# Two blocks on one core: the second blocks' softmax division on ScalarE, and merged masks in the third branch

## The chip, the cores and the metric

The kernel runs on one core of a Trainium2 chip. The metric is the device time of one launch in microseconds. Engines are called as in the profile: PE (TensorE, matmuls; PEld its weight loads), DVE (VectorE), ACT (ScalarE), POOL (GpSimd), SP (the queue that issues most DMAs).

## The reference

The input has 512 tokens of width 1024 in float32. A first block (differential attention, multiscale pooling, a two-level mixture of experts) is followed by two layers of a second kind of block. Each of these layers projects the normed input and feeds three branches side by side: a gated delta rule ("gdn"), a latent attention with 6 heads ("mla") and a linear recurrence with decay ("rwkv", called the third branch here). Their outputs are gated, joined and multiplied with `w_out_2`, and added to the residual.

Two pieces of it matter here. The latent attention is, per head, softmax(q kT) v over 512 tokens. With blocks of 128 queries that is 4 x 6 = 24 units per layer, each with a 128x512 matrix of weights that is divided by its row sums. The third branch is computed in chunks of 64 tokens: inside a chunk, products of keys and queries with keys are masked to a triangle, and a unit lower triangular system of each chunk is solved.

## The kernel before, in words

After the first block (until about 1000 us) come the two layers, one after the other. The Python code that builds the program has generators for the branches; `weave` interleaves them, and what it settles is the order of PE's instructions, which is kept as it is written. The orders of DVE, ACT, POOL and SP come from the scheduler of the framework, which places each instruction where its own simulated times put it. So a change of one instruction's engine or size can move others on these engines. All engines run their instructions in order: one that waits holds up those behind it.

The stretch of the change is where the third branch's `prepare` and then its `states` are woven with `mla`.

*The third branch, `products` (L1922 to L1967).* For each of two directions and four token tiles, 16 small matmuls fill the PSUM tile `x2`, one half for each parity of head (`par`). DVE then writes `SC` (the products times the mask `mk`) and `RB` (the products times `m2`): before, one instruction for each parity, so four instructions a tile. 16 matmuls with `SC` follow, whose results ACT copies to `AKV` (L1963) and DVE adds to `YK` (L1967). There are 8 such tiles a layer, 16 in all. The last three of a layer lie inside the solve.

*The third branch, the solve (L1990 to L2006).* The triangular systems go through DRAM into the layout `au`, and DVE solves them by 30 pairs of instructions, `stmp` (L1342, a product of two parts of `au`) and `au` (L1344, a subtraction), each waiting for the one before. The solution goes through DRAM again into `XT` and `LT`, is transposed by DVE (L2004, L2006), and the matmuls of `off_diagonal` follow, then `states`.

*The latent attention (`mla`, L2152 on).* `scores(n)` for a unit: one matmul into a PSUM tile `mm`; DVE takes the negated row maximum `nm` (L2233); ACT computes `e = exp(scores + nm)` and the row sums `rs` (L2236, with a second small instruction that reads the sums out); DVE takes the reciprocal of `rs` (L2237); POOL multiplies `e` by it (L2238). `turn(n)` transposes the scaled `e` by four matmuls (L159), and ACT copies the result to `t2` (L2246). `outputs` multiplies `t2` of two heads with the values into `mo`. `scores` runs three units ahead of `turn`, and three PSUM tiles serve both in turn, so a new `scores` also needs an older `t2` copy to be done.

When the last unit is done, `Mix` takes over the memory of the attention and loads `w_out_2`, the gate and the branch outputs.

Of the kernel before, what the change touches and what calls it, by code (L numbers as in the profile page):

```python
# [12 lines left out]
AF = mybir.ActivationFunctionType  # L13
ALU = mybir.AluOpType
# [76 lines left out]
def half(p):  # L91
    return slice(64 * p, 64 * p + 64)
# [6 lines left out]
def tok(t):  # L99
    return slice(128 * t, 128 * t + 128)  # L100
# [1648 lines left out]
class Rwkv:  # L1749
# [54 lines left out]
    def prepare(self, mud, xud):  # L1804
        net, a, l, rw, tc, nc = self.net, self.a, self.l, self.rw, self.net.tc, self.net.nc
# [8 lines left out]
        RB = pl.tile([128, 2, 16, 64], F32, name="RB")  # L1814
# [6 lines left out]
        with pool(tc, "rka", 1, "right") as tmp, pool(tc, "rks", 2, "right") as small, pool(tc, "rpa", 1, "right", PSUM) as psum:  # L1821
# [102 lines left out]
            def products(d):  # L1924

                BB = BBs[d]
                m1 = net.const("stf64" if d == 0 else "stb64")
                m2 = net.const("inf64" if d == 0 else "inb64")
                mk = small.tile([128, 128], F32, name="mk", bufs=1)
                nc.gpsimd.tensor_copy(mk[:, 0:64], m1)  # L1930
                nc.gpsimd.tensor_copy(mk[:, 64:128], m2)
                for t in range(NT):
                    us = slice(4 * t, 4 * t + 4)
                    yield 1.2
                    ps = psum.tile([128, 2, 512], F32, name="x2", bufs=1)
                    for par in range(2):
                        for cp in range(2):
                            for i in range(2):
                                for c in range(2):
                                    o, f = cp * 192 + i * 64, 64 - 64 * i  # L1940
                                    ts = slice(t * 128 + c * 64, t * 128 + c * 64 + 64)
                                    net.matmul(ps[half(c), par, o:o + 128 - f], BB[half(par), i, cp, ts],
                                                     KR[half(par), d, cp, 2 * t + c, f:], start=True, stop=True)
                    pv = ps[:, :, :384].rearrange("p a (c k) -> p a c k", c=2)
                    SC = small.tile([128, 2, 2, 128], F32, name="SC")
                    for par in range(2):
                        nc.vector.tensor_tensor(SC[:, par], pv[:, par, :, 64:], mk[:, None, :].to_broadcast([128, 2, 128]), op=ALU.mult)
                    for par in range(2):
                        nc.vector.tensor_tensor(RB[:, d, us].rearrange("p (a c) k -> p a c k", a=2)[:, par], pv[:, par, :, 0:64],
                                                m2[:, None, :].to_broadcast([128, 2, 64]), op=ALU.mult)  # L1950
                    SU = SC.rearrange("p a c k -> p (a c) k")
                    yield 1.5
                    pv = psum.tile([128, 512], F32, name="mm", bufs=2)
                    for u in range(4):
                        h = 2 * (u % 2) + u // 2
                        for j in range(2):
                            for c in range(2):
                                net.matmul(pv[half(c), 256 * j + u * 64:256 * j + u * 64 + 64], SU[half(c), u, 64 * j:64 * j + 64],
                                           vt[half(c), t, h * 64:h * 64 + 64], start=True, stop=True)
                    pvv = pv.rearrange("p (x u k) -> p x u k", x=2, u=4)  # L1960
                    for c in range(2):
                        st = 2 * t + c if d == 0 else 7 - 2 * t - c
                        nc.scalar.activation(AKV[half(c), st], pvv[half(c), 0], AF.Copy)  # L1963
                    if d == 0:
                        nc.scalar.activation(YK[:, t], pvv[:, 1], AF.Copy)
                    else:
                        nc.vector.tensor_tensor(YK[:, t], pvv[:, 1], YK[:, t], op=ALU.add)  # L1967
# [42 lines left out]
            def rest():  # L2010
                yield from triangles(0)
                yield from products(0)
                while 1 not in BBs:
                    yield 1
                yield from products(1)
                yield from bonus()
# [132 lines left out]
def mla(net, a, l, mchd, mixt, tabd):  # L2149

    tc, nc = net.tc, net.nc
    with ExitStack() as ctx:  # L2152
# [75 lines left out]
        def scores(n):  # L2228
            t, h = units[n]
            ps = psum.tile([128, 512], F32, name="mm", bufs=3)  # L2230
            net.matmul(ps, qT[:, h, tok(t)], kT[:, h], start=True, stop=True)
            nm = tmp.tile([128, 1], F32, name="nm")
            nc.vector.tensor_reduce(nm, ps, AX.X, ALU.max, negate=True)  # L2233
            e = es[n] = tmp.tile([128, S], F32, name="e", tag="t1", bufs=4)
            rs = tmp.tile([128, 1], F32, name="rs")
            nc.scalar.activation(e, ps, AF.Exp, bias=nm, accum_out=rs)  # L2236
            nc.vector.reciprocal(rs, rs)  # L2237
            nc.gpsimd.tensor_scalar(e, e, rs, None, op0=ALU.mult)  # L2238

        def turn(n):  # L2240
            e = es.pop(n)
# [22 lines left out]
        for n in range(3):  # L2264
            scores(n)
        yield 0.8
        for n in range(len(units) + 1):
            if n < len(units):
                turn(n)
                yield 0  # L2270
            if n + 3 < len(units):
                scores(n + 3)
                yield 0
            if n and n % 2 == 0:
                outputs(n - 2)
                yield 0
# [262 lines left out]
```

## Time and profile before

| | us |
|---|---|
| median of 3 runs | 1907.91 |
| lowest and highest run | 1902.60, 1915.12 |
| the profiled execution's own time | 1903.25 |
| its span, first to last instruction | 1901.5 |
| busy: PE, DVE, ACT, POOL | 1653.5, 1046.3, 583.7, 558.4 |

A page of the profile gives busy times by engine, the chain of work that ended last, and the costliest groups of instructions with a mean time of one. The trace behind it can be asked for stretches of time (windows), for who waited for whom, and for instructions in order (timeline). A row like `L2238 POOL TENSOR_SCALAR e<-e,rs` names the line, the engine, the operation, and output and inputs by the program's names. "idle before <-X" is time in which the engine had nothing to run, and X what ended it.

### The profile page before, as it was taken

Reading aid. Unit: us, or ns where it says so; the run is one execution under the profiler, and the core shown is the slowest. Engines: PE = TensorE matmul, PEld = TensorE weight load, DVE = VectorE, ACT = ScalarE, POOL = GpSimd, SP = SyncE. Lnnn points to the kernel's source line nnn. Section 1 sums busy time; section 2 is a strip of 40 time slices with the busy share of each in tenths; the row PEclk is TensorE's granted clock in tenths of the full one; section 3 lists DMA queues with packets and bytes.
Section 4 is the critical chain, followed back from the end, with each engine's and each line's share of the span. In section 5 each row is a group of like instructions: output and inputs, shape, how many; then the busy total and the mean of one; then the engine's idle time right before and its main releaser. Section 6 shows DMA issues by size and latency. Waiting matters only on the chain.

```text
span 1901.5 us, 34119 instructions
## 1 busy us (share of the span) xinstructions
PE 1653.5 (87%) x14010; PEld 1100.7 (58%) x14010; DVE 1046.3 (55%) x2224; ACT 583.7 (31%) x1154; POOL 558.4 (29%) x559
## 2 busy tenths in 40 slices
PE   5999998999999999959978968777789799789776
PEld 3986584444444444438756755455577577545554
DVE  2435534344434333355895567836656875678456
ACT  4344432212121212144432124331344331244212
POOL 1113111000000000025651243454335721354443
PEclk8899998999999999979988989898889999989888
DMA  9934726999999999833424120123433441201332
GB/s 310 238 107 139 257 74 221 393 392 398 399 406 400 392 399 396 308 102 95 106 68 99 62 73 21 30 93 106 133 84 94 112 111 50 53 33 39 99 111 89
DMA packets 243219, 337.10 MB, mean 177 GB/s; under 512 B 92769, under 2 KB 166161, under 8 KB 226225
## 3 DMA queue, kind: packets, MB, share of 16 engines
q1 hardware_dynamic: 241152, 329.88, 50.3%
q10 hardware_dynamic: 1152, 3.22, 0.5%
q8 instruction: 112, 1.84, 0.4%
q0 software_dynamic: 752, 1.76, 0.3%
q14 instruction: 51, 0.41, 0.1%
HBM read 310.84 MB, written 23.99 MB: 176 GB/s over the span
## 4 chain that ended last, share of the span: by engine, by line
PE 25%; DVE 17%; DMA 5%; issue 4%; POOL 3%; ACT 2%; SPq 1%; DVEq 0%; POOLq 0%; ACTq 0%
PE mm L149 17%; DVE stmp L1342 2%; DVE au L1344 2%; PE mm L159 2%; PE tr L149 1%; PE x L149 1%; PE pu L149 1%; PE kp L149 1%; DMA w<-in_w_out_dram 1%; DMA au<-mud 1%; DVE nm L2233 1%; DVE y L1293 1%; PE mo L149 1%; DMA gate<-gated 1%; POOL w L2310 1%
## 5 line engine op out<-in xcount | busy, mean ns | idle before, releaser
L149 PE MATMUL gu<-w,XT 128*64 128x512 f32 x1024 | 225.8, 594 | 0.0
L149 PE MATMUL mm<-hh,wh 128*128 128x512 f32 (+1 forms) x464 | 203.9, 440 | 0.0
L149 PE MATMUL mm<-hh,wl 128*128 128x512 f32 (+1 forms) x464 | 188.4, 406 | 0.0
L149 PE MATMUL mm<-hl,wh 128*128 128x512 f32 (+1 forms) x464 | 188.1, 405 | 0.0
L928 POOL TENSOR_TENSOR yl<-y,yh 128x512 fp32r<-128x512 f32 x30 | 38.1, 1270 | 451.4 <-ACT yh L927 451.4
L149 PEld LDWEIGHTS gu<-w,XT 128*64 128x64 f32 x1024 | 72.1, 137 | 142.7 <-issue 136.2
L938 DVE TENSOR_TENSOR xres<-mm,xres 128x512 f32<-128x512 f32 x128 | 79.2, 681 | 90.7 <-PE mm L149 90.7
L149 PE MATMUL mm<-w,hT 128*64 128x512 f32 x512 | 113.4, 595 | 0.7 <-ACT hT L912 0.7
L149 PE MATMUL mm<-w,mh 128*128 128x512 f32 x256 | 92.9, 442 | 22.8 <-POOL w L2310 10.0
L149 PEld LDWEIGHTS mm<-hh,wh 128*128 128x128 f32 (+1 forms) x464 | 91.6, 198 | 26.6 <-issue 3.5
L149 PEld LDWEIGHTS mm<-hh,wl 128*128 128x128 f32 (+1 forms) x464 | 91.1, 196 | 21.0
L149 PEld LDWEIGHTS mm<-hl,wh 128*128 128x128 f32 (+1 forms) x464 | 91.8, 198 | 19.1 <-DVE hl L1162 0.2
L1214 ACT ACTIVATE wh<-w 128x1024 fp32r<-128x1024 f32 (+1 forms) x54 | 57.0, 1056 | 145.8 <-PE mm L149 105.9
L1216 POOL TENSOR_TENSOR wl<-w,wh 128x1024 fp32r<-128x1024 f32 (+1 forms) x28 | 69.4, 2478 | 110.0 <-ACT wh L1214 91.3
L149 PE MATMUL mm<-wh,hh 128*128 128x256 f32 x320 | 93.8, 293 | 2.2 <-ACT hh L357 2.2
L149 PE MATMUL mm<-wh,hl 128*128 128x256 f32 x320 | 91.0, 284 | 4.3 <-DVE hl L359 4.0
L2238 POOL TENSOR_SCALAR e<-e,rs 128x512 f32<-128x512 f32 x48 | 75.5, 1574 | 65.3 <-DVE rs L2237 59.8
L149 PE MATMUL mm<-wl,hh 128*128 128x256 f32 x320 | 90.6, 283 | 1.6 <-DVE wl L381 1.6
L149 PEld LDWEIGHTS mm<-w,hT 128*64 128x64 f32 x512 | 35.3, 137 | 66.6 <-issue 62.5
L149 PEld LDWEIGHTS mm<-w,mh 128*128 128x128 f32 x256 | 50.1, 206 | 41.1 <-POOL w L2310 12.5
L1342 DVE TENSOR_TENSOR stmp<-au 96x60 f32<-96x60 f32 (+29 forms) x120 | 64.5, 537 | 14.3 <-DMA au<-rmud 6.5
L872 ACT ACTIVATE X<-mm,ws 128x512 f32<-128x512 f32 x32 | 22.0, 688 | 151.4 <-DVE ws L869 128.1
(580 smaller groups left out, 3596.3 us busy)
## 6 DMA issues: line engine op xcount, KB each, us to landing
w<-in_w_gate_dram SPq DMA_DIRECT2D x64, 1024.0 KB, 13.2
w<-in_w_up_dram SPq DMA_DIRECT2D x64, 1024.0 KB, 13.4
w<-in_w_down_dram SPq DMA_DIRECT2D x64, 1024.0 KB, 10.0
w<-in_w_in_dram SPq DMA_DIRECT2D x52, 512.0 KB, 4.1
w<-in_w_ada_dram SPq DMA_DIRECT2D x24, 1024.0 KB, 8.5
w<-in_w_out_dram SPq DMA_DIRECT2D x16, 512.0 KB, 3.8
w<-in_w_in_dram SPq DMA_DIRECT2D x6, 1024.0 KB, 12.1
w<-in_w_out_dram SPq DMA_DIRECT2D x4, 1024.0 KB, 6.3
```

The costliest lines, as they stand in the source:

```text
L149: return self.nc.tensor.matmul(out, a, b, **kw)
L159: return self.nc.tensor.transpose(out, a, ident)
L872: nc.scalar.activation(X[:, 512 * i:512 * i + 512], ps, AF.Copy, scale=ws[:, 1:2])
L928: (nc.vector if last else nc.gpsimd).tensor_tensor(yl[:, hs], y, yh[:, hs].bitcast(F32), op=ALU.subtract)
L938: nc.vector.tensor_tensor(net.xres[:, t, hs], po, net.xres[:, t, hs], op=ALU.add)
L1214: nc.scalar.activation(h[:, :, :m], w[:, :, :m], AF.Copy)
L1216: eng.tensor_tensor(lo[:, :, :m], w[:, :, :m], h[:, :, :m].bitcast(F32), op=ALU.subtract)
L1293: nc.vector.scalar_tensor_tensor(y[:, lo:hi], ps[:, lo + d:hi + d], cw[:, j, m:m + 1], y[:, lo:hi], op0=ALU.mult, op1=ALU.add)
L1342: nc.vector.tensor_tensor(tv, au[:n, :, j + 1:, j:j + 1].to_broadcast(sh), au[:n, :, j:j + 1, 0:j].to_broadcast(sh), op=ALU.mult)
L1344: nc.vector.tensor_tensor(au[:n, :, j + 1:, 0:j], au[:n, :, j + 1:, 0:j], tv, op=ALU.add)
L2233: nc.vector.tensor_reduce(nm, ps, AX.X, ALU.max, negate=True)
L2238: nc.gpsimd.tensor_scalar(e, e, rs, None, op0=ALU.mult)
```

## The change

Two edits. In `products`, the two instructions for `SC` become one of 128x512 elements, and the two for `RB` one of 128x256. In `scores`, the multiplication of `e` by the reciprocal sums leaves POOL and becomes an ACT instruction, a copy with a scale of one value per partition, in place.

```diff
--- before.py
+++ after.py
@@ -1943,11 +1943,9 @@
                                                      KR[half(par), d, cp, 2 * t + c, f:], start=True, stop=True)
                     pv = ps[:, :, :384].rearrange("p a (c k) -> p a c k", c=2)
                     SC = small.tile([128, 2, 2, 128], F32, name="SC")
-                    for par in range(2):
-                        nc.vector.tensor_tensor(SC[:, par], pv[:, par, :, 64:], mk[:, None, :].to_broadcast([128, 2, 128]), op=ALU.mult)
-                    for par in range(2):
-                        nc.vector.tensor_tensor(RB[:, d, us].rearrange("p (a c) k -> p a c k", a=2)[:, par], pv[:, par, :, 0:64],
-                                                m2[:, None, :].to_broadcast([128, 2, 64]), op=ALU.mult)
+                    nc.vector.tensor_tensor(SC, pv[:, :, :, 64:], mk[:, None, None, :].to_broadcast([128, 2, 2, 128]), op=ALU.mult)
+                    nc.vector.tensor_tensor(RB[:, d, us].rearrange("p (a c) k -> p a c k", a=2), pv[:, :, :, 0:64],
+                                            m2[:, None, None, :].to_broadcast([128, 2, 2, 64]), op=ALU.mult)
                     SU = SC.rearrange("p a c k -> p (a c) k")
                     yield 1.5
                     pv = psum.tile([128, 512], F32, name="mm", bufs=2)
@@ -2235,7 +2233,7 @@
             rs = tmp.tile([128, 1], F32, name="rs")
             nc.scalar.activation(e, ps, AF.Exp, bias=nm, accum_out=rs)
             nc.vector.reciprocal(rs, rs)
-            nc.gpsimd.tensor_scalar(e, e, rs, None, op0=ALU.mult)
+            nc.scalar.activation(e, e, AF.Copy, scale=rs)
 
         def turn(n):
             e = es.pop(n)
```

The diff shifts line numbers by 2: the exp is L2234, the new ACT multiplication L2236 and the copy to `t2` L2244 in the changed program.

PE's order is the same in both programs, instruction for instruction. The schedulers' orders of the others differ. First ACT, in the first of the two layers, from the first exp of `mla` on. Before:

```order
L2236 ACTIVATE e_11016,rs_11017<-mm_11012,nm_11014 128x512
L2236 ACTIVATE e_11025,rs_11026<-mm_11021,nm_11023 128x512
L2236 ACTIVATE e_11034,rs_11035<-mm_11030,nm_11032 128x512
L2246 ACTIVATE t2_11066<-mm_11061 128x512
L2236 ACTIVATE e_11072,rs_11073<-mm_11068,nm_11070 128x512
L2246 ACTIVATE t2_11082<-mm_11077 128x512
L1963 ACTIVATE AKV_9799<-mm_11084 64x256 x2
L2246 ACTIVATE t2_11118<-mm_11113 128x512
```

and now:

```order
L2234 ACTIVATE e_11006,rs_11007<-mm_11002,nm_11004 128x512
L2236 ACTIVATE e_11006<-e_11006,rs_11007 128x512
L2234 ACTIVATE e_11015,rs_11016<-mm_11011,nm_11013 128x512
L2236 ACTIVATE e_11015<-e_11015,rs_11016 128x512
L2234 ACTIVATE e_11024,rs_11025<-mm_11020,nm_11022 128x512
L2236 ACTIVATE e_11024<-e_11024,rs_11025 128x512
L2244 ACTIVATE t2_11054<-mm_11049 128x512
L2234 ACTIVATE e_11060,rs_11061<-mm_11056,nm_11058 128x512
L2244 ACTIVATE t2_11070<-mm_11065 128x512
L2236 ACTIVATE e_11060<-e_11060,rs_11061 128x512
L1961 ACTIVATE AKV_9799<-mm_11072 64x256 x2
L2244 ACTIVATE t2_11106<-mm_11101 128x512
```

Each exp is followed, one to three instructions later, by the multiplication of the same `e`. The copy `t2` of the first unit, which came behind three exps, now comes behind three exps and three multiplications.

Second DVE, in the second layer, at the beginning of the solve. Before, from the last instruction ahead of that piece:

```order
L1967 TENSOR_TENSOR YK_14990<-mm_16182,YK_14990 128x256
L2233 TENSOR_REDUCE nm_16204<-mm_16202 128x1
L1342 TENSOR_TENSOR stmp_16062<-au_15999 128x30
L2233 TENSOR_REDUCE nm_16213<-mm_16211 128x1
L1344 TENSOR_TENSOR au_15999<-au_15999,stmp_16062 128x30
L2237 RECIPROCAL rs_16207<-rs_16207 128x1
L2233 TENSOR_REDUCE nm_16222<-mm_16220 128x1
L1342 TENSOR_TENSOR stmp_16065<-au_15999 128x58
L2237 RECIPROCAL rs_16216<-rs_16216 128x1
L1344 TENSOR_TENSOR au_15999<-au_15999,stmp_16065 128x29x2
L1342 TENSOR_TENSOR stmp_16068<-au_15999 128x84
L1344 TENSOR_TENSOR au_15999<-au_15999,stmp_16068 128x28x3
```

and now, where five rows of the solve (`stmp`, `au`, `stmp`, `au`, `stmp`, for widths 30, 58 and 84) stand ahead of the first row shown:

```order
L1344 TENSOR_TENSOR au_15975<-au_15975,stmp_16042 128x28x3
L1342 TENSOR_TENSOR stmp_16045<-au_15975 128x108
L1344 TENSOR_TENSOR au_15975<-au_15975,stmp_16045 128x27x4
L1342 TENSOR_TENSOR stmp_16048<-au_15975 128x130
L1344 TENSOR_TENSOR au_15975<-au_15975,stmp_16048 128x26x5
L1965 TENSOR_TENSOR YK_14974<-mm_16156,YK_14974 128x256
L1342 TENSOR_TENSOR stmp_16051<-au_15975 128x150
L2231 TENSOR_REDUCE nm_16178<-mm_16176 128x1
L1344 TENSOR_TENSOR au_15975<-au_15975,stmp_16051 128x25x6
L2231 TENSOR_REDUCE nm_16187<-mm_16185 128x1
L1342 TENSOR_TENSOR stmp_16054<-au_15975 128x168
L2235 RECIPROCAL rs_16181<-rs_16181 128x1
```

The row maxima `nm` of the first units stood among the first three steps of the solve. Now the first of them stands behind five whole pairs, `YK` and a sixth `stmp`; in the first layer it stood, and stands, behind six pairs, `YK` and a seventh `stmp`. From the first pair to the last, the solve of the second layer has 13 row maxima in both programs, that of the first layer 9 in both.

On POOL, the 48 multiplications are gone and nothing else moves there but one pair of instructions; on SP, one DMA issue changes places with another, twice. In the second layer's projection, some DVE instructions (`wl`, `rw`) move by a few steps of an earlier solve.

## Rows read from the trace of the kernel before

**Rows 1.** Page, part 4: shares of the chain that ended last, by engine.

```profile
PE 25%; DVE 17%; DMA 5%; issue 4%; POOL 3%; ACT 2%; SPq 1%; DVEq 0%; POOLq 0%; ACTq 0%
```

**Rows 2.** Windows: stretch, length; busy us (instructions) of PE, PEld, DVE, ACT, POOL; PEclk; DMA; GB/s.

```profile
1190.80:1223.40 32.60, 22.00 (x256) 14.60 (x254) 30.60 (x93) 12.60 (x31) 12.92 (x9) 0.90 0.00 1
1223.40:1248.50 25.10, 20.76 (x384) 13.16 (x384) 13.46 (x30) 11.17 (x27) 17.22 (x14) 0.93 0.30 70
1248.50:1274.10 25.60, 22.87 (x396) 15.78 (x391) 11.56 (x27) 10.78 (x23) 14.20 (x18) 1.00 0.15 51
1720.20:1755.60 35.40, 31.14 (x330) 20.77 (x328) 33.86 (x103) 17.96 (x44) 20.69 (x14) 0.95 0.03 7
1755.60:1772.00 16.40, 11.73 (x308) 8.33 (x306) 8.73 (x17) 5.21 (x13) 11.27 (x12) 0.79 0.39 94
1772.00:1797.60 25.60, 22.84 (x400) 15.76 (x388) 11.55 (x27) 10.78 (x23) 12.32 (x14) 1.00 0.15 51
```

**Rows 3.** Lines, whole run: instructions xcount | busy us, mean ns | idle before <-releaser.

```profile
L2238 POOL TENSOR_SCALAR e<-e,rs 128x512 f32<-128x512 f32 x48 | 75.5, 1574 | 65.3 <-DVE rs L2237 59.8
L2236 ACT ACTIVATE e<-mm,nm 128x512 f32<-128x512 f32 x48 | 33.0, 687 | 62.9 <-DVE nm L2233 61.2 <-DVE au L1344 1.0 <-DVE rs L2237 0.6
L2246 ACT ACTIVATE t<-mm 128x512 f32<-128x512 f32 x48 | 28.1, 593 | 19.1 <-PE mm L159 18.4
L872 ACT ACTIVATE X<-mm,ws 128x512 f32<-128x512 f32 x32 | 22.0, 688 | 151.4 <-DVE ws L869 128.1 <-DVE ws L871 13.4 <-PE mm L149 9.9
L927 ACT ACTIVATE yh<-y 128x512 fp32r<-128x512 f32 x32 | 20.2, 630 | 87.0 <-DVE y L926 84.1 <-DVE n L2141 3.0
L1947 DVE TENSOR_TENSOR SC<-x,mk 128x256 f32<-128x256 f32 x32 | 12.0, 416 | 7.6 <-PE x L149 7.4
L1949 DVE TENSOR_TENSOR RB<-x,cst 128x128 f32<-128x128 f32 x32 | 7.6, 279 | 0.0
```

**Rows 4.** Waits of PE: us, times, longest. First row 1186:1276, others 1715:1798.

```profile
PE mm L159 <- POOL e L2238: 10.2, 2, 7.4
...
PE mm L149 <- DVE XT L2006: 4.6, 2, 2.5
PE mm L159 <- POOL e L2238: 3.0, 2, 2.7
```

**Rows 5.** Timeline, DVE, then POOL: start us, us, instruction.

```profile
1197.16 0.50 DVE L1342 TENSOR_TENSOR stmp<-au 128x198 f32<-128x198 f32 x1
1197.69 0.37 DVE L1344 TENSOR_TENSOR au<-au,stmp 128x198 f32<-128x198 f32 x1
...
1200.52 0.77 DVE L1342 TENSOR_TENSOR stmp<-au 128x228 f32<-128x228 f32 x1
1201.32 0.40 DVE L1344 TENSOR_TENSOR au<-au,stmp 128x228 f32<-128x228 f32 x1
...
1750.69 0.69 DVE L1342 TENSOR_TENSOR stmp<-au 128x150 f32<-128x150 f32 x1
1751.41 0.32 DVE L1344 TENSOR_TENSOR au<-au,stmp 128x150 f32<-128x150 f32 x1
...
1198.64 3.27 POOL L2238 TENSOR_SCALAR e<-e,rs 128x512 f32<-128x512 f32 x2 [0.31 <-DVE rs L2237]
```

**Rows 6.** Timeline: first solve rows and first transposes of both layers, then two output groups.

```profile
1190.85 0.20 DVE L1342 TENSOR_TENSOR stmp<-au 128x30 f32<-128x30 f32 x1 [4.46 <-DMA au<-rmud]
1198.39 1.12 PE L159 MATMUL mm<-cst,e 128*128 128x128 f32 x4 [7.45 <-POOL e L2238]
...
1720.20 0.20 DVE L1342 TENSOR_TENSOR stmp<-au 128x30 f32<-128x30 f32 x1 [2.09 <-DMA au<-rmud]
1722.92 0.66 PE L159 MATMUL mm<-cst,e 128*128 128x128 f32 x4 [2.68 <-POOL e L2238]
...
1234.95 1.54 PE L149 MATMUL mo<-t,vt 128*64 128x128 f32 x16
...
1239.17 1.09 PE L149 MATMUL mo<-t,vt 128*64 128x128 f32 x16
```

## The prediction

> **What bounds the kernel now.** I read the page first, then stretches of time around the two layers' attention, then waits and the timeline in them. The chain of waits is shared: PE holds a quarter of the span, DVE a sixth, POOL 3% and ACT 2% [rows 1]. So the reader should not ask which engine is busiest over the whole run, but which one ends last where the change is made. That is two stretches of about 80 us, one in each layer; the first 1000 us are not touched.
>
> The windows cut each of them into three [rows 2]. While the third branch's solve runs, DVE is busy 30.6 of 32.6 us in the first layer and 33.9 of 35.4 in the second: it is full, with the solve's 60 small instructions and the attention's row maxima and reciprocals in one queue. PE is busy 22.0 of 32.6, and 31.1 of 35.4. In the next window, which ends with the first matmuls of the states, PE works off attention units. In the last one PE goes through a fixed mixture of units and states, 25.6 us in both layers, and POOL's work does not show there as a wait.
>
> The two layers differ in who is late when the solve is done. In the second layer PE stood 4.6 us waiting for the transposed solution (`XT`) [rows 4]: the solve was late. In the first layer that wait doesn't occur; there PE waited 10.2 us in two places for POOL's `e` [rows 4], one of 7.4 us before the first transposes, and PE was late. The reason can be seen in the timeline: the first transposes come 7.5 us after the solve's first row in the first layer (1198.39 - 1190.85), but 2.7 us in the second (1722.92 - 1720.20) [rows 6], since DVE's queue has the row maxima behind the first pairs of the solve in the one and among them in the other.
>
> **The change, part by part.**
>
> *POOL loses 48 multiplications of 1.574 us* [rows 3]. What that gives at the spot: for PE, the way from the reciprocal to the transposes is shorter by 1.574 less the new ACT instruction. That one reads SBUF with a scale from a tile. The nearest rows are a copy with such a scale but out of PSUM, 0.688 us, and a copy out of SBUF without one, 0.630 [rows 3]. I take 0.69; the lower bound is the plain copy's 0.593, the upper one 0.725, the SBUF row plus what the scale adds (0.688 - 0.593). So the way is 0.88 us shorter. PE waits for it four times [rows 4]. The first wait of the first layer is followed by a stretch in which DVE sets the pace, so 0.88 earlier is worth nothing there; the second, of 2.8 us (10.2 - 7.4), is worth 0.88. The two of the second layer lie before the solve's end, where PE was early anyway: nothing.
>
> *DVE gets rid of a disturbance.* Just after POOL begins one of these multiplications, a solve instruction in DVE takes longer: 0.50 us where its neighbour of the same width takes 0.37, 0.77 against 0.40, 0.69 against 0.32 [rows 5]. In the first layer's solve there are six such instructions (the first at 1197.16), in the second's seven (the last at 1750.69); against the same widths elsewhere they lose 0.13 to 0.50 us each, 2.2 us and 3.0 us in all. DVE is full there and the solve is one chain, so this comes off the solve.
>
> The Trainium skill (GPSIMD Engine Reference, Key points) says that POOL shares its SBUF interfaces with DVE, and that DVE instructions with two SBUF inputs contend with it; the solve's are of that kind. By that rule I would have looked for every such instruction beside POOL to be slow. The trace shows it for one at a time near a POOL start: two POOL multiplications ran for 3.27 us from 1198.64, and 0.77 us at 1200.52 is followed by an undisturbed 0.40 at 1201.32 [rows 5]. By the rule the gain would be larger, by the rows it is 5.2; I take the rows.
>
> *The masks.* `SC` takes 0.416 us for 256 elements a partition, `RB` 0.279 for 128 [rows 3]; so 128 elements cost 0.137 and an instruction 0.142 besides. Two into one saves 0.142, so 0.28 a tile, 4.5 us of DVE in 16 tiles. Three tiles a layer lie in the solve where DVE is full: 0.85 a layer. The other five lie before the solve, among longer waits between PE, ACT and DVE; and the matmuls that follow could begin after the first half of `SC`, and now begin 0.27 us later (0.137 x 2). I count these at nothing, with bounds of 2.8 us (10 x 0.28) to either side.
>
> *ACT gets 33 us more* (48 x 0.69). While the solve runs it was busy 12.6 of 32.6 us and 18.0 of 35.4 [rows 2], so it has room. After the solve PE runs units back to back: two units took 4.2 us (1239.17 - 1234.95) [rows 6]. ACT needs for two: 2 x (0.687 + 0.593 + 0.69) = 3.94, with reading out the sums on top. This fits only just, and now `t2` copies stand behind multiplications that wait for DVE's reciprocals. I charge 1 us a layer; what more it could be is a rival below.
>
> *The order in the second layer.* The row maxima now come as late as in the first layer, one pair of the solve earlier (0.65 us, by widths between those of [rows 5]). The first transposes should thus come 7.5 - 0.88 - 0.65 = 6.0 us after the solve's start instead of 2.7: PE is 3.3 us later. Its slack was 4.6.
>
> **The sum.** First layer: PE is late and follows DVE, which is freed by 2.2 + 0.85 = 3.05, plus 0.88 at the second wait: 3.9. Second layer: the solve ends 3.0 + 0.85 = 3.85 earlier, PE comes 3.3 later, so the slack of 4.6 becomes 4.6 - 3.3 - 3.85 = -2.55, PE is now the late one, and the stage gains 4.6 - 3.3 = 1.3; with the units carried along by a freer DVE up to 3.85. I take 2. Both, less 1 us each for ACT: 3.9 + 2 - 2 = 4 us off. What comes after a stretch (loading `w_out_2` and so on) starts when the last unit is done and moves with it, so nothing further hides this.
>
> The profiled execution took 1903.25 us (its span is 1901.5), so the sum gives 1899. That execution lay 4.7 us below the median of the runs, and the median itself lies in a spread of 12.5, so I forecast between the two ways of taking it off: **1902 us**, that is no change by the bound of 1% (19 us), about what a measurement of this kernel can tell from no change.
>
> **The rivals.**
>
> *A larger gain.* All of PE's waits for POOL go (13.2 us [rows 4]), and the later units of the second layer are carried along. For it: the waits are at the head of each stretch, and all that follows on PE is in fixed order. Against: while DVE is full, PE arrives earlier only to wait for row maxima. With 3.85 in the second layer, 3.05 in the first, 2.6 of the waits that I counted at nothing (3 x 0.88), 2.8 of the masks and 1 to 3 more of disturbance outside the solve: about 14 us, 1894. Chance 0.18.
>
> *Slower: ACT's queue takes POOL's place.* Place: the ten or so units of each layer that PE runs back to back around the solve's end. ACT's multiplication must wait for the reciprocal, which DVE takes after ACT has read out the sums; this gap of some 0.45 us an `e` (an estimate, the reading's place between the exp's end and the reciprocal) was filled on POOL's side before, and now stops ACT, with the next `t2` behind it. Then two units need 3.94 + 0.9 = 4.84 us against PE's 4.2: 0.64 a pair, 3.2 us a layer. With the 3.3 us of the second layer's late start also on the path, and only the first layer's solve helping, it comes to 6.4 + 3.3 - 3 = 7 us more: 1915 from the median. It decides from the point where ACT needs more than 4.2 us for two units. For it: the sum above stands within 7% of that. Against: the scheduler has put another exp or copy between most exps and their multiplications. Chance 0.17.
>
> *Nothing moves.* DVE's freed time turns into waits of DVE for PE and ACT, and the reordering takes what the disturbance gave: 1907. The spans before are equal to within 6 us although the two layers were ordered so differently (83.3 us from the solve's start to the last unit in the first, 77.4 in the second, from the windows' edges [rows 2]): the order alone is worth up to 5.9 us, and the second layer could take on the first one's length less 3.9. Chance 0.15.
>
> **Chances and range.** Forecast (1 to 9 us off) 0.5, larger gain 0.18, nothing 0.15, slower 0.17. Only the far ends of the second and the last pass 1%: faster by over 1% 0.04, slower by over 1% 0.04, within 1% 0.92. The range takes in the larger gain's lower half, 1890, and most of the slower case, 1913.
>
> **What would show it.** Right: in the solve windows, no `stmp` or `au` above its width's usual time; the first layer's solve at 29 to 30 us instead of 32.6, the second's at 31 to 32; PE's wait for `XT` in the second layer gone or under 1 us; the new ACT instruction at 0.66 to 0.73; last windows still 25.6 us. Wrong: a wait of PE for ACT's `e` or `t2` of several us after the solve; disturbed solve instructions although POOL is idle; the second layer's stretch longer than 77.4 us.

## The result and the profile after

The changed kernel takes 1917.72 us (median of 7 runs, 1915.95 to 1921.42) against 1908.15 for the kernel before (7 runs, 1902.6 to 1915.12): ratio 1.0055, 95% interval 1.0039 to 1.0072. It is about 10 us slower. The forecast was 1902, with a range up to 1913. The profiled execution has a span of 1914.2 us and took 1915.95, the lowest of its runs, so its trace stands at the fast edge of what it explains.

The chain of waits (page, part 4, shares by engine) has shifted a little from DVE and POOL to PE, and ACT's share is what it was [rows 1]:

```profile
PE 27%; DVE 16%; DMA 5%; issue 3%; ACT 2%; POOL 2%; SPq 1%; DVEq 0%; POOLq 0%; ACTq 0%
```

The same windows as [rows 2], cut at the same places of the work (solve; up to the states; units and states), first and second layer. Columns as there; the one before the last two is PE's granted clock:

```profile
1193.80:1226.40 32.60, 29.12 (x290) 19.17 (x286) 28.77 (x86) 18.45 (x40) 0.16 (x1) 0.74 0.01 2
1226.40:1251.80 25.40, 21.67 (x390) 13.68 (x392) 13.82 (x31) 17.72 (x39) 3.63 (x7) 1.00 0.30 68
1251.80:1277.40 25.60, 23.02 (x399) 15.91 (x399) 11.57 (x27) 14.78 (x29) 3.06 (x8) 1.00 0.16 51
1731.90:1766.30 34.40, 30.19 (x337) 20.30 (x336) 30.62 (x95) 23.66 (x51) 0.16 (x1) 0.90 0.02 7
1766.30:1785.10 18.80, 14.76 (x332) 9.74 (x332) 10.26 (x21) 11.66 (x25) 3.60 (x7) 0.82 0.34 82
1785.10:1810.70 25.60, 23.02 (x414) 15.91 (x404) 11.57 (x27) 14.78 (x29) 3.05 (x8) 1.00 0.15 52
```

POOL is empty in the solve (12.92 and 20.69 us before, 0.16 now) and DVE is less full (30.6 to 28.8, 33.9 to 30.6). Yet the stretches are not shorter: 83.6 us against 83.3 in the first layer, 78.8 against 77.4 in the second. Both together cost 1.7 us. The larger part of the loss must lie elsewhere.

PE runs its 14,010 matmuls in the same order in both kernels (but for four neighbours that change places near 1279 and near 1802), so their starts can be compared one by one. In this pair of executions the changed one is 4.8 us late at 1502 and 12.9 us late at 1556; at the end it is 12.7 us late. So 8 us come in at one place in the second layer's projection, the sixth pair of `rw` (L1318, L1319). DVE there, first in the kernel before (start, length, instruction):

```profile
1547.53 0.75 DVE L1318 SCALAR_TENSOR_TENSOR rw<-mm,smalls,rw 128x511 f32<-128x511 f32 x1 [2.29 <-ACT rw L1317]
1548.31 0.75 DVE L1319 SCALAR_TENSOR_TENSOR rw<-mm,smalls,rw 128x511 f32<-128x511 f32 x1
1553.19 3.94 DVE L1633 STREAM_TRANSPOSE LT<-XT 32x768 f32<-32x768 f32 x4 [4.12 <-DMA XT<-xud]
```

and the same instructions in the changed kernel, with the matmuls on PE that wait for them in the last row:

```profile
1556.37 1.95 DVE L1633 STREAM_TRANSPOSE LT<-XT 32x768 f32<-32x768 f32 x2 [5.60 <-DMA XT<-xud]
1558.36 0.75 DVE L1318 SCALAR_TENSOR_TENSOR rw<-mm,smalls,rw 128x511 f32<-128x511 f32 x1
1559.13 1.96 DVE L1633 STREAM_TRANSPOSE LT<-XT 32x768 f32<-32x768 f32 x2
1561.12 0.97 DVE L1635 STREAM_TRANSPOSE XT<-LT 32x768 f32<-32x768 f32 x1
1562.12 0.75 DVE L1319 SCALAR_TENSOR_TENSOR rw<-mm,smalls,rw 128x511 f32<-128x511 f32 x1
...
1563.02 0.87 PE L159 MATMUL tr<-cst,rw 128*128 128x128 f32 x3 [5.20 <-DVE rw L1319]
```

Before, DVE finished the pair and then stood 4.12 us waiting for the DMA of `XT`; nobody missed it. Now the transposes stand ahead of the pair. The pair's input was there (PE was already on the next columns), but DVE takes its queue in order, so the pair waits for a DMA that has nothing to do with it, and PE stands 5.2 us. Behind the pause PE runs at half speed for a while. Windows of the 5.6 us from the transposes of `rw` on, the changed kernel, then the one before:

```profile
1563.00:1568.60 5.60, 5.58 (x17) 4.62 (x18) 3.52 (x4) 1.71 (x3) 0.00 (x0) 0.50 0.35 94
```

```profile
1552.70:1558.30 5.60, 5.60 (x30) 4.70 (x29) 5.02 (x5) 1.43 (x3) 0.00 (x0) 1.00 0.98 189
```

The granted clock is 0.50 (1.2 GHz) against 1.00, and 17 matmuls are done instead of 30; that is the other 2 to 3 us. The change edits neither `rw` nor the transposes: the scheduler, which orders each engine's queue by its own estimate of times, now has them the other way round, although the nearest divisions end some 280 us before this place and begin some 170 us behind it.

### The profile page after: what moved, and what is told of

Read it like the earlier page. It is cut to its first block, busy times and chain, and to the rows that moved or that the text cites. A ratio compares the mean times of both kernels' runs of the same rounds, so it can differ in the third digit from the quotient of the medians.

```text
span 1914.2 us, 33950 instructions
## 1 busy us (share of the span) xinstructions
PE 1676.0 (88%) x14010; PEld 1117.7 (58%) x14010; DVE 1042.2 (54%) x2192; ACT 615.6 (32%) x1202; POOL 481.2 (25%) x511
## 4 chain that ended last, share of the span: by engine, by line
PE 27%; DVE 16%; DMA 5%; issue 3%; ACT 2%; POOL 2%; SPq 1%; DVEq 0%; POOLq 0%; ACTq 0%
PE mm L149 18%; DVE stmp L1342 2%; DVE au L1344 2%; PE mm L159 2%; PE x L149 2%; PE tr L149 1%; PE pu L149 1%; PE kp L149 1%; PE mo L149 1%; DMA w<-in_w_out_dram 1%; DMA au<-mud 1%; DVE y L1293 1%; DMA gate<-gated 1%; POOL w L2308 1%; DVE wl L1216 1%
## 5 line engine op out<-in xcount | busy, mean ns | idle before, releaser
L926 DVE SCALAR_TENSOR_TENSOR y<-mm,ws,g2b 128x512 f32<-128x512 f32 x32 | 24.0, 751 | 78.2 <-PE mm L149 78.2
```

The lines of the kernel that those rows point to most:

```text
L926: nc.vector.scalar_tensor_tensor(y, py, ws[:, 0:1], net.g2b[:, hs], op0=ALU.mult, op1=ALU.mult)
```

## Experiments

An added edge of the kind `NoSync` only tells the scheduler which of two instructions of DVE comes first; it adds no semaphore. `ORDER` stands for it. "After" is the changed kernel. Each ratio is to runs of the kernel before on the same chip in the same session, whose medians were 1907.51 (runs 1 to 4), 1905.33 (5 to 8) and 1906.19 (9 to 11). `net.turned` holds the transposes, `net.begun` the first instruction of the solve; the lines that set them are left out of the cuts of code below.

**1 and 2. Each half alone.**

```diff
-            nc.gpsimd.tensor_scalar(e, e, rs, None, op0=ALU.mult)      # run 1: this
+            nc.scalar.activation(e, e, AF.Copy, scale=rs)
-                    for par in range(2):                               # run 2: only these
-                        nc.vector.tensor_tensor(SC[:, par], ...)
+                    nc.vector.tensor_tensor(SC, ...)                   # and RB likewise
```

> The kernel before with only the division moved to ScalarE; the masks stay four instructions. Its DVE order has the sixth pair of rw in the second layer's projection between and behind the LT transposes, as the whole change has. Theory A (the order of rw): most of the loss comes with this half, 1914 to 1918 us, and the trace shows PE waiting some 5 us for rw near 1555. Theory B (ScalarE's queue holds the divisions back in the two attention stretches): also 1914 to 1918, but with no such wait near 1555, the loss lying between 1190 and 1280 and between 1720 and 1810. If the division is harmless and the masks did it: 1906 to 1909.

> The kernel before with only the masks merged, two instructions for four; the division stays on POOL. Its DVE order keeps the sixth rw pair of the second layer's projection ahead of the LT transposes. Theory A and theory B alike: no loss, 1905 to 1909 us, and no wait of PE for rw near 1553 over 2 us in the second layer. If the masks' half has a share in the loss (its instruction of 512 elements standing in the way of the solve): 1910 to 1914.

Division alone: 1918.09 us, ratio 1.0061 (1.0039 to 1.0084), and a wait of PE for `rw` of 7.6 us. Masks alone: 1905.87, 0.9996 (0.9977 to 1.0015), no such wait. The whole loss comes with the division, and the wait is where theory A put it. This doesn't yet tell how much of the loss is the order's and how much ScalarE's queue.

**3. The order of `rw` put back.**

```diff
-            nc.vector.scalar_tensor_tensor(y[:, :S - 1], ...)
+            i = nc.vector.scalar_tensor_tensor(y[:, :S - 1], ...)
+            if m == 5 and self.l == 1:
+                [net.tc.add_manual_dep(t, i.ins.name, ORDER) for t in net.turned]   # the four L1633
```

> The changed kernel with one thing added: in the second layer's projection the four LT transposes (L1633) must stand behind the sixth rw pair (L1318, L1319) on DVE, as they do in the kernel before. Nothing else of DVE's order moves but one pair of instructions later on. Theory A (the order of rw costs 5.3 us of waiting and some 3 us of lower clock behind it): 1909 to 1911 us, no wait of PE for rw over 1 us near 1555, and the starts of PE's instructions from there on 7 to 9 us earlier against the changed kernel. Theory B (ScalarE's queue): 1916 to 1919.

1913.37 us, ratio 1.0023 (0.9998 to 1.0048). Some 6 of the 10 us come back, and 4 stay, so it falls between what the two theories expected. At the place itself the trace shows what theory A said (DVE, then PE):

```profile
1550.93 0.75 DVE L1319 SCALAR_TENSOR_TENSOR rw<-mm,smalls,rw 128x511 f32<-128x511 f32 x1
1553.99 3.94 DVE L1633 STREAM_TRANSPOSE LT<-XT 32x768 f32<-32x768 f32 x4 [2.31 <-DMA XT<-xud]
...
1555.26 0.60 PE L159 MATMUL tr<-cst,rw 128*128 128x128 f32 x4
```

No wait. PE's lead over the changed kernel's trace grows from some 2 to 10 us around this place; some 6 us of that are lost by 1600, where the clock of this execution falls (0.78 from 1575 to 1610, against 0.95 in the trace of before), and at the end of the two traces the lead is 6.0.

**4. The order of `rw` spoiled in the kernel before.**

```diff
+            if m == 5 and self.l == 1:
+                net.tc.add_manual_dep(i.ins, net.turned.name, ORDER)   # L1319 behind the last L1633
```

> The kernel before with one thing added: in the second layer's projection the second instruction of the sixth rw pair (L1319) must stand behind the four LT transposes on DVE. The scheduler also moves some instructions of the second layer's attention stretch by a few places. Theory A: the wait of PE for rw appears near 1553, 3 to 5.5 us, and the time is 1911 to 1917 us. Theory B (nothing but ScalarE's work matters): 1906 to 1909.

1931.88 us, ratio 1.0140 (1.0113 to 1.0167): slower than both theories said. The wait is there, with POOL still dividing:

```profile
1552.57 3.94 DVE L1633 STREAM_TRANSPOSE LT<-XT 32x768 f32<-32x768 f32 x4 [5.32 <-DMA XT<-xud]
1556.54 0.75 DVE L1319 SCALAR_TENSOR_TENSOR rw<-mm,smalls,rw 128x511 f32<-128x511 f32 x1
...
1557.43 0.87 PE L159 MATMUL tr<-cst,rw 128*128 128x128 f32 x3 [5.55 <-DVE rw L1319]
```

The rest of its loss was the finding that led on. The edge had made the scheduler move the first row maximum `nm` of the second layer's attention behind 15 instructions of the solve, and the solve waits for a DMA of its own. DVE and PE there:

```profile
1726.00 0.21 DVE L1342 TENSOR_TENSOR stmp<-au 128x30 f32<-128x30 f32 x1 [4.23 <-DMA au<-rmud]
...
1730.80 0.68 DVE L2233 TENSOR_REDUCE nm<-mm 128x1 f32<-128x512 f32 x1
...
1734.42 1.11 PE L159 MATMUL mm<-cst,e 128*128 128x128 f32 x4 [8.10 <-POOL e L2238]
```

That layer's stretch became 92.2 us long, from 77.4 [rows 2]. The row names POOL as the releaser, but POOL was only the last link: `nm` had come late. It is not the first one alone: by DVE's order in this trace, only 6 row maxima stand between the first and the last pair of this solve, where the kernel before has 13. So this run spoils more than the pair of `rw`, and its 24 us are no measure of that pair. The changed kernel has the same thing in small: its first `nm` stands behind eleven instructions of the solve (not ten, as the expectation of run 5 has it), where in the kernel before it ran 2.8 us ahead of the solve (1717.44). The changed kernel, DVE and PE:

```profile
1731.98 0.20 DVE L1342 TENSOR_TENSOR stmp<-au 128x30 f32<-128x30 f32 x1 [4.15 <-DMA au<-rmud]
...
1735.32 0.68 DVE L2231 TENSOR_REDUCE nm<-mm 128x1 f32<-128x512 f32 x1
...
1738.36 1.11 PE L159 MATMUL mm<-cst,e 128*128 128x128 f32 x4 [4.21 <-ACT e L2236]
```

**5. That order put back, too**, on top of the edit of run 3.

```diff
+            i = nc.vector.tensor_reduce(nm, ps, AX.X, ALU.max, negate=True)
+            if n == 0 and l == 1:
+                net.tc.add_manual_dep(net.begun, i.ins.name, ORDER)    # the solve's first L1342 behind it
```

> The changed kernel with two orders set on DVE in the second layer: the LT transposes (L1633) behind the sixth rw pair, as in the run with that alone, and the first instruction of the solve of the attention stretch (L1342) behind the first maximum of scores (nm, L2231), which is where the kernel before has it; in the changed kernel the first nm stands behind ten instructions of the solve, which wait for the DMA of au. Theory A2 (what is left of the loss is that nm waits behind the solve's DMA): 1907 to 1911 us, PE's wait for the first transposes of the second layer's attention down from 4.2 to under 2.5 us. Rival (the rest of the loss is ScalarE's extra 33 us): 1912 to 1915, as with the rw order alone.

1908.43 us, ratio 1.0014 (0.9997 to 1.0032). PE's wait for the first transposes is 2.1 us instead of 4.2, and the second layer's stretch 76.5 instead of 78.8. With both orders of the kernel before, the difference to it is no longer told from none; but it is not the gain that was forecast either (4 us off would be a ratio of 0.998). The step from run 3 to this one (1.0023 to 1.0014) is smaller than the intervals; the trace shows it, the times alone don't.

**6 to 8. Both orders in both layers, without and with the change.** In the first layer both kernels have the pair of `rw` behind the transposes and `nm` behind the solve, so there was something to gain for both.

> The kernel before with one order set on DVE: in the first layer's projection, too, the LT transposes stand behind the sixth rw pair (in the second layer they do already). If the wait of 4.2 us for rw in the first layer (trace of before, 960 to 1130) lies on the path to the end: 1902 to 1905 us. If a later wait takes it up (the solve of the first attention stretch, which waits for a DMA of its own): 1906 to 1909.

> The changed kernel with both orders set in both layers: rw ahead of the LT transposes, the first nm ahead of the solve. If waits behind a DMA on DVE are what cost time: 1896 to 1906 us, faster than the kernel before. If ScalarE's extra work is what costs: 1909 to 1914.

> The kernel before with the same two orders set in both layers; the division stays on POOL and the masks stay four instructions. The difference to the changed kernel with these orders is what the division and the masks are worth by themselves, the order held alike. By the working of the prediction the changed one is 4 us faster (1902 to 1908 here against 1896 to 1906); if ScalarE's work costs more than POOL's saved, this one is the faster by 2 us or more.

Run 6 (kernel before, `rw` first in the first layer too): 1905.44 us, 1.0002 (0.9985 to 1.0019), between the two expectations. PE's wait of 4.2 us for `rw` is gone, but at the next transposes PE now waits for ACT's copy `vt` (L1775), 1.4 us here and 3.7 us in run 8. PE is 6.7 us earlier at 1036 than in the trace of before; runs 2 and 4, without this order, are 6.1 and 7.1 us earlier there as well, so this is not its doing. None of it is left at 1186; most goes around 1160, where matmuls start 1.01 us apart that are 0.53 apart in the trace of before (half clock). By the times, a wait of the same size was worth some 6 us in one layer (run 3) and nothing in the other, to within some 3 us.

Run 7 (changed kernel, all four orders): 1900.05 us, 0.9967 (0.9951 to 0.9984). It is faster than both kernels, and 8 us under run 5, from which it differs by the first layer's two orders alone. Run 8 (kernel before, all four): 1903.15 us, 0.9985 (0.9966 to 1.0003). Solve windows and the ones behind them, run 7, first and second layer:

```profile
1189.60:1221.00 31.40, 27.45 (x324) 17.72 (x324) 29.55 (x92) 21.98 (x47) 0.00 (x0) 1.00 0.03 8
1221.00:1241.30 20.30, 16.51 (x349) 10.55 (x346) 10.82 (x24) 13.31 (x30) 3.59 (x7) 0.92 0.34 76
...
1716.90:1750.60 33.70, 32.56 (x367) 21.42 (x366) 31.65 (x99) 27.22 (x59) 0.17 (x1) 1.00 0.03 8
1750.60:1765.30 14.70, 9.36 (x297) 7.01 (x298) 8.13 (x16) 6.69 (x15) 3.58 (x7) 0.77 0.48 104
```

and run 8:

```profile
1190.80:1225.60 34.80, 31.87 (x331) 20.47 (x330) 32.45 (x100) 15.88 (x38) 15.83 (x10) 0.85 0.02 7
1225.60:1244.50 18.90, 15.72 (x344) 10.43 (x343) 10.56 (x22) 8.59 (x20) 13.86 (x12) 0.91 0.34 82
...
1721.40:1756.80 35.40, 33.58 (x362) 21.82 (x360) 33.85 (x103) 18.48 (x46) 20.71 (x14) 0.95 0.03 7
1756.80:1773.00 16.20, 11.45 (x310) 8.01 (x308) 8.76 (x18) 5.24 (x13) 11.05 (x12) 0.79 0.39 94
```

With the orders alike, the changed kernel's two windows are 51.7 us against 53.7 in the first layer and 48.4 against 51.6 in the second: 2.0 and 3.2 us shorter, with ACT busier and POOL idle. Part of this is clock (1.00 against 0.85 and 0.95 in the solve windows). The medians differ by 3.1 us; the two intervals overlap a little, so a gain is likely, but not shown beyond the spread. The two traces may overstate it: run 7's execution took 1898.15 us, 2 below its median, run 8's 1907.26, 4 above.

**9 to 11. What each order and half is worth.** Run 9 leaves `rw` as the changed kernel has it; run 10 puts `n < 3` for `n == 0`; run 11 is run 7 with the masks as four instructions.

> The changed kernel with the first nm ahead of the solve in both layers, and rw left where the changed kernel has it (behind LT transposes in both layers). If the two orders act each by itself: the 7 to 9 us that the rw order was worth are missing against the run with all four orders set, 1904 to 1909 us, with PE's wait of 5 us for rw in the second layer back. If the nm order alone gives the whole gain: 1898 to 1902.

> The changed kernel with all four orders set, and the second and third maximum of scores (nm) ahead of the solve as well. Waits behind a DMA: the first transposes start earlier still in the first layer (PE waited 2.2 us for e there with one nm ahead), 1896 to 1900 us. If the solve sets the end and the three nm (0.68 us each) only delay it: 1900 to 1904.

> The division on ScalarE alone, masks as four instructions, with the four orders set. Splits the difference of some 3 us between the two kernels with the orders set: by the prediction's terms (2.2 to 3.0 us a layer for the division, 0.85 a layer for the masks, 2 us of charge) it lies some 2 us above the run with the masks merged too, 1900 to 1903.

Run 9: 1902.89, 0.9984 (0.9964 to 1.0004), between the two expectations. PE's waits for `rw` are back in the second layer (3.5 us at a matmul and 3.5 at the transposes behind it), yet the kernel is no slower than the one before, and only some 3 us slower than run 7. So the two orders don't add: the pair was worth some 6 us in run 3, where `nm` was late, and 3 here. The trace of run 7 shows what takes up the rest. With the pair out of the way, PE stands at the next transposes of `rw` for ACT's copy `vt`, and `vt` stands in ACT's queue behind a `wh` that waited for the DMA of a weight (ACT, then PE):

```profile
1547.66 1.06 ACT L1214 ACTIVATE wh<-w 128x1024 fp32r<-128x1024 f32 x1 [5.95 <-DMA w<-in_w_in_dram]
...
1549.20 0.59 ACT L1775 ACTIVATE vt<-tr 128x512 f32<-128x512 f32 x1
...
1549.84 1.12 PE L159 MATMUL tr<-cst,rw 128*128 128x128 f32 x4 [4.50 <-ACT vt L1775]
```

Run 10: 1901.33, 0.9983 (0.9959 to 1.0006), no better than run 7. Run 11: 1904.59, 0.9993 (0.9977 to 1.0010), over the 1900 to 1903 expected: the division without the masks is not told from run 8. What run 7 has over run 8 can't be put down to the division by these times; the masks may hold most of it, although alone (run 2) they gave nothing.

## Why the prediction was wrong

**The step that failed** is the reading of the place: "two stretches of about 80 us, one in each layer". The list of moved instructions included "some DVE instructions (`wl`, `rw`)" in the second layer's projection. They were said to move "by a few steps" and got no price in the sum. I never asked what those rows were moved behind. They were moved behind a transpose that waits for a DMA, and the trace of before had the size: DVE stood 4.12 us at that transpose. Put back, this one pair gives some 6 of the 10 us (run 3, between intervals of several us). That share holds beside a late `nm`: with `nm` ahead of the solve in both layers and the pair left behind the transposes, no loss to the kernel before is left (run 9).

**The order in the second layer's attention** was seen and its mechanism was right: first transposes 6.0 us after the solve's start, measured 6.4 (1738.36 - 1731.98). The price was off. I set it against a slack of 4.6 us and let 2 us of gain remain; but PE's order is one queue too. PE stood 4.2 us, and then DVE, whose queue has the maxima of later units among the solve's instructions, waited 1.2 us for PE's scores and 1.0 us in three places for ACT. So the solve's window took 34.4 us instead of the 31 to 32 forecast, PE still waited 2.4 us for `XT` (under 1 forecast), and the stretch grew by 1.4.

**The gain from POOL's silence** is partly there. No solve instruction near the old places is stretched any more; the changed kernel's trace, to be held against [rows 5]:

```profile
1200.14 0.35 DVE L1342 TENSOR_TENSOR stmp<-au 128x198 f32<-128x198 f32 x1
...
1203.36 0.40 DVE L1342 TENSOR_TENSOR stmp<-au 128x228 f32<-128x228 f32 x1
```

0.50 became 0.35, and 0.77 became 0.40, as the widths' usual times had it. That agrees with the Trainium skill (GPSIMD Engine Reference, Key points), by which DVE instructions with two SBUF inputs contend with POOL. The term was too large: the solve's 60 instructions took 21.3 us together in the first layer and 22.1 in the second before, 19.7 and 19.6 now, so 1.6 and 2.5 less where 2.2 and 3.0 were taken. And the first layer's solve still took 32.6 us, not 29 to 30: in this execution PE ran at 0.74 of its clock there (0.90 before) and DVE had gaps waiting for it. In run 3, whose DVE order in that solve is the same, the window is 30.8 us at a clock of 0.78, and in run 5 it is 30.7:

```profile
1193.60:1224.40 30.80, 23.16 (x251) 16.08 (x247) 28.69 (x87) 17.82 (x38) 0.17 (x1) 0.78 0.01 2
```

So 1.8 of the 3.05 us for that solve show in these two executions. In run 1, which has the division without the masks, the window is 34.0 us at a clock of 0.70. In these four executions the window goes with PE's clock in it, which differs from one execution to the next.

**ScalarE's rival** (1915) came nearest in time and was wrong in place. The multiplication took 0.718 us (0.69 taken, 0.725 the upper bound); PE's waits for `e` in the first layer come to 3.9 us with the longest, 2.3, at the first transposes, and only 1.6 lie behind the solve; for `t` it waits 0.3. The groups of the changed kernel:

```profile
L2236 ACT ACTIVATE e<-e,rs 128x512 f32<-128x512 f32 x48 | 34.2, 718 | 7.6 <-DVE rs L2235 7.4
L2244 ACT ACTIVATE t<-mm 128x512 f32<-128x512 f32 x48 | 28.0, 590 | 11.4 <-PE mm L159 11.1
L1946 DVE TENSOR_TENSOR SC<-x,mk 128x512 f32<-128x512 f32 x16 | 11.0, 689 | 9.8 <-PE x L149 9.7
L1947 DVE TENSOR_TENSOR RB<-x,cst 128x256 f32<-128x256 f32 x16 | 6.6, 414 | 0.0
```

The gap of ACT before the multiplication that I feared is 7.4 us over 48, not 0.45 each. The last windows are 25.6 us as forecast. The masks cost 0.689 and 0.414 us, so 0.287 a tile is saved, as worked out (0.28).

**The sum failed apart from the pair, too.** With the pair put back and `nm` where the prediction had it, the kernel should have been 4 us faster than the one before; it is some 4 us slower (run 3, -0.4 to +9). With `nm` put back as well it is 3 us slower (run 5, -0.6 to +6). Both intervals leave out 4 us faster. In run 5's trace the stretches themselves are shorter than before, 81.6 us against 83.3 and 76.5 against 77.4. Both stretches of run 5:

```profile
1187.30:1268.90 81.60, 67.45 (x1036) 45.24 (x1036) 53.89 (x144) 49.89 (x104) 6.84 (x16) 0.92 0.15 38
1722.30:1798.80 76.50, 66.51 (x1030) 45.45 (x1030) 51.68 (x141) 48.96 (x102) 6.81 (x16) 0.91 0.14 40
```

But its first stretch ends 5.2 us earlier than in the trace of before (1268.9, 1274.1), and its second begins 2.1 us later (1722.3, 1720.2). Run 8, with the division on POOL, goes from 4.0 us ahead at the end of its second window (1244.5, 1248.5) to 1.2 behind (1721.4, 1720.2). So the step "nothing further hides this" does not hold for the first layer: what is saved there is used up in the work between the stretches. Part of that is clock, and waits for a weight's DMA as in run 7 are one way; how much each takes, single traces don't tell.

Only with all four orders set do the medians differ as the sum had it (4 us forecast, 3.1 between runs 8 and 7). That arrangement is neither kernel's, so this agreement is luck more than proof of the terms. Whether ScalarE's extra work has a share in the 3 to 4 us that runs 3 and 5 leave stays open.

## What to carry to other kernels

When a scheduler sets the order, the diff of the queues is the change: go through every moved instruction on the path, far from the edit too, and ask what it now stands behind and whether that waits for a DMA or another engine. An instruction that waits harmlessly for 4 us in the trace of before is a trap for whatever is put behind it. Measure an edit's own worth with such orders pinned alike in both versions, and say which orders: here the same edit cost 10 us as scheduled and some 3 with the second layer's orders of the kernel before, and gained some 3 with both orders set in both layers, the last two at the edge of the spread. For the changed kernel the order was worth more than the edit. And a gain inside a stretch is not yet a gain in time: ask what the work behind it waits for, a weight's DMA for one.

## What the runs showed of the hardware

In 89 timed executions of the kernel before, the mean granted clock lay between 0.917 and 0.933 and went with the time (correlation -0.77): 26 runs from 0.918 up to 0.922 had a median of 1910.2 us, 41 runs from 0.926 on 1903.6. So a good part of its spread of 19 us (1897.51 to 1916.87 in one session) goes with the clock. Where the clock falls is not set by the program alone: a pause of PE of 2.09 us near 1158, the same in the traces of both kernels, was followed by 10 us at half clock in the changed one and by none in the one before. The changed kernel, PE and a window:

```profile
1158.71 0.74 PE L159 MATMUL mm<-cst,s 128*128 128x128 f32 x4 [2.09 <-DVE s L1876]
...
1159.10:1169.30 10.20, 10.20 (x79) 6.46 (x78) 2.95 (x5) 3.59 (x7) 2.54 (x2) 0.50 0.00 0
```

and the kernel before:

```profile
1158.47 0.63 PE L159 MATMUL mm<-cst,s 128*128 128x128 f32 x4 [2.09 <-DVE s L1876]
...
1158.90:1169.10 10.20, 10.20 (x123) 6.36 (x122) 6.89 (x12) 6.11 (x12) 3.79 (x3) 1.00 0.01 2
```

What decides it, these traces don't tell. For readers of traces it means that a difference of 3 to 5 us between two single executions proves nothing until a wait is found that explains it.
